# Later S5 and convolution steps, joined transposes and one shared last block in a two-layer hybrid encoder trunk

## The chip, the cores and the metric

The kernel runs on one core of one Trainium2 chip. The metric is the device time of one execution in microseconds (us), taken as the median of several runs. TensorE is called PE here, VectorE DVE, ScalarE ACT, GpSimd POOL and SyncE SP, as in the profile.

## The reference, cut to what matters

```python
for l in range(2):                                   # x: 256 tokens x 1024 channels, float32
    x = x + 0.5 * swiglu(rmsnorm(x), w_gate, w_up, w_down)      # d_ff = 2816
    h = rmsnorm(x); p = h @ w_in                     # 2048 branch columns, 4096 gate columns
    y_a = s5_mixer(u_a)        # block-diagonal complex scan, gelu, glu
    y_b = pool_mixer(u_b)      # trailing means over 2, 4, 8, 16 tokens, one 64x64 product each
    y_c = rwkv7_mixer(...)     # delta-rule state, here in chunks of 64 tokens
    y_d = b_g * conv3(c_g * z_in)
    merged = sum over g of sigmoid(gate_g) * (y_g @ w_branch[g])
    x = x + merged @ w_out
    x = x + 0.5 * swiglu(rmsnorm(x), w_gate, w_up, w_down)
return rmsnorm(x)
```

swiglu(h) is (silu(h @ w_gate) * (h @ w_up)) @ w_down.

## The kernel before

**The large products.** The 256 tokens are two token tiles t of 128. Each weight matrix comes from HBM in units of 128 x 1024 numbers (`raw`, five buffers, issued on SP). A unit is split into two float32r parts: ACT writes the rounded part `wh` (line 250), DVE the rest `wl` (line 225, called from `Unit.finish`). The activations are split in the same way into `xh` and `xl` (or `hh`, `hl` behind the feed-forward's middle, `yh`, `yl` of a branch, and `mo`). One step of the contraction over 128 rows for one token tile, called a k-step below, is three matmuls (lines 256 to 258): `wh` by `xh`, `wl` by `xh`, `wh` by `xl`, each 512 columns wide. A unit normally serves four k-steps: two k for two token tiles.

**The order.** `Flow` lays out the whole instruction order by hand when the program is built. The list of its steps holds the large products, two k-steps in each. All else hangs on generators ("threads") that wait for a place in that list: `wA(n)` runs n steps later ahead of the products, `wB(n, banks)` n steps later behind them, `wM(n, banks)` and `wT(n)` after n k-steps, at most one `M` thread for each k-step. `banks` is the number of free PSUM banks that it also asks for. Four PSUM banks of tag `pb` serve all small products, and are handed out in turn (names such as `gm`, `tmA`, `sT`, `inv`). Each engine then works through its own list strictly in that order.

**Feed-forward (`ffn`).** The columns of w_gate and w_up go in blocks of 512; since 2816 is 5 x 512 + 256, the last block of each is 256 wide, in units of four k. `act` applies silu to a gate block, `hid` multiplies it with the up block into `hd`, turns `hd` on PE with four transposes (line 268), and splits the result into `hh` and `hl`. `down` multiplies these with w_down; at its end `next_input` adds to `x`, turns each half of `x` with four transposes (line 268), and writes the scaled halves `xg`, `xh`, `xl` for the next stage. In `hid` and `next_input` the transposes of a token tile follow one step after its result, and the two token tiles end one step apart.

**Mixer (`mixer`).** `cols` multiplies the branch columns, and four threads work beside the large products: `rwkv`, `conv`, `s5`, `pool`. In `s5` the steps on PE are `sT`, `sS`, `sY` and `glu`; on DVE they are the chain `gA`, `gt`, `gB` with two scans (line 1372), then `Hs`. In `conv` the product `zc` of `cg` and `z_in` is followed by the taps `cv` (line 1497). In `rwkv` PE makes `gm` (from `W` and `BK`), turns `W` and `KB` into `tmA` and `tmB`, makes `akv`, and then climbs a ladder of four rungs that inverts a triangular matrix: `inv` from `Tm` and `Bl`, copied by ACT to `Xm`, then `inv` from `Xm` and `Rd`, which DVE adds to `Tm` and turns into `Rd` again. `Gm` is the masked `gm`, `RH` and `UV` are copies of `tmA`. The gates and the projections of the branches (`gate_steps(b)`, `branch_steps(b)`, summed in `mg`) follow in the order 3 (conv), 1 (pool), 0 (S5), 2 (RWKV).

Of the kernel before, what the change touches and what calls it, by code (L numbers as in the profile page):

```python
# [50 lines left out]
def wA(n=1):  # L51

    return ("A", n, 0)
# [7 lines left out]
def wB(n=0, banks=0):  # L61

    return ("B", n, banks)
# [7 lines left out]
def wM(n=1, banks=0):  # L71

    return ("M", n, banks)


class Flow:
# [19 lines left out]
    def spawn(self, gen):  # L96
        self.threads.append([None, gen])
        self._advance(self.threads[-1])
# [73 lines left out]
def trunk_kernel(ctx: ExitStack, tc: tile.TileContext, a, out, dbg=None):  # L172
    nc = tc.nc
    ve, sc, gp, pe = nc.vector, nc.scalar, nc.gpsimd, nc.tensor
    sp = nc.sync
# [12 lines left out]
    spawn = fl.spawn  # L188
# [15 lines left out]
    def xs(tl, t):  # L204
        return tl[:, :, t * 128:(t + 1) * 128]
# [7 lines left out]
    def free(n=1):  # L213
        fl.banks += n
        assert fl.banks <= NB
# [14 lines left out]
    class Unit:  # L230


        def __init__(self, W, k0, nk, c0, n, eng=ve):
            self.spec = (W, k0, nk, c0, n)
            self.k0, self.nk, self.eng = k0, nk, eng

        def can_load(self):
            return True
# [1 line left out]
        def load(self):  # L240
            W, k0, nk, c0, n = self.spec
            self.r = block(raw, nk, n, F32, "raw")
            sp.dma_start(out=self.r,
                         in_=W[k0 * 128:(k0 + nk) * 128, c0:c0 + n].rearrange("(k p) f -> p k f", p=128))

        def convert(self):
            W, k0, nk, c0, n = self.spec
# [12 lines left out]
    def mmu(ps, lh, ll, u, ktot):  # L260
        for k in range(u.nk):
            kk = u.k0 + k
            mm3(ps, lh(kk), ll(kk), u.h[:, k], u.l[:, k], kk == 0, kk == ktot - 1)
            fl.tick()
# [5 lines left out]
    def lxh(t):  # L270
        return lambda k: xh[:, k, t * 128:(t + 1) * 128]

    def lxl(t):
        return lambda k: xl[:, k, t * 128:(t + 1) * 128]


    rstd = {}
# [19 lines left out]
    def next_input(t, hf, p, scale, ss, gain):  # L297

        if p is not None:
            yield wA(1)
            update(t, hf, p, scale)
        yield wB(1 if p is not None else 0, 1)
        b = bank()
        transposes(b, x[t][:, hf * 512:(hf + 1) * 512], 4)
        yield wA(1)
        xg = scr.tile([128, 4, 128], F32, name="xg", tag="xg", bufs=2)
        r, n = vrow[gain[0]]
        r += gain[1] * n + 4 * hf  # L310
        tt(xg, b.rearrange("p (a q) -> p a q", q=128), vec[:, r:r + 4].unsqueeze(2).to_broadcast([128, 4, 128]))
        free()
        dh, dl = xs(xh, t)[:, 4 * hf:4 * hf + 4], xs(xl, t)[:, 4 * hf:4 * hf + 4]
        sc.activation(dh, xg, AF.Copy)  # L314
        yield wT(1)
        tt(dl, xg, dh.bitcast(F32), ALU.subtract)
        yield wA(1 if p is not None else 4)
        square_sum(t, hf, ss)
        if hf:
            rsqrt_mean(t, ss)  # L320
# [72 lines left out]
    def ffn(l, which, final=False, extra=None, first=None):  # L393
        Wg, Wu, Wd = (a[f"ffn{which}_w_{n}"][l] for n in ("gate", "up", "down"))
        st = {}
        es = ExitStack()

        def enter():
            fp = es.enter_context(tc.tile_pool(name=f"ffn{l}{which}", bufs=1))
            st["fp"] = fp  # L400
            st["hh"] = [fp.tile([128, F // 128, 128], F32R, name=f"hh{t}") for t in range(2)]
            st["hl"] = [fp.tile([128, F // 128, 128], F32R, name=f"hl{t}") for t in range(2)]
            if final:
                fin["pool"] = fp
                fin["pre"] = {}
                fin["gb"] = fp.tile([128, D], F32, name="gb")
                sp.dma_start(out=fin["gb"], in_=a["final_norm"].partition_broadcast(128))
            if first:
                first(fp)
            if extra:  # L410
                spawn(extra(fp))

        fl.step(enter, work=False)
        if first:
            for _ in range(4):
                fl.step(fl.tick)

        def act(t, pg, n, sl):
            yield wA(1)
            sg = st["fp"].tile([128, 512], F32, name="sg", tag="sg", bufs=2)  # L420
            sc.activation(sg[:, :n], pg[:, :n], AF.Silu, scale=rstd[t])  # L421
            sl[t] = sg

        def hid(t, pu, c0, n, sl):
            yield wA(1)
            sg = sl[t]
            hd = st["fp"].tile([128, 512], F32, name="hd", tag="hd", bufs=2)
            ve.scalar_tensor_tensor(out=hd[:, :n], in0=pu[:, :n], scalar=rstd[t], in1=sg[:, :n],  # L428
                                    op0=ALU.mult, op1=ALU.mult)
            k0, nk = c0 // 128, n // 128  # L430
            yield wB(1, 1)
            b = bank()
            transposes(b, hd, nk)
            yield wA(1)
            split(st["hh"][t][:, k0:k0 + nk], st["hl"][t][:, k0:k0 + nk],
                  b[:, :n].rearrange("p (a q) -> p a q", q=128))
            free()

        for c0 in range(0, F, 512):
            n = min(512, F - c0)  # L440
            P, sl = {}, {}

            def go(w, t, u, P=P, sl=sl, c0=c0, n=n):
                def f():
                    if (w, t) not in P:
                        P[w, t] = acc()
                    mmu(P[w, t][:, :n], lxh(t), lxl(t), u, 8)
                    if u.k0 + u.nk == 8:
                        spawn(act(t, P[w, t], n, sl) if w == 0 else hid(t, P[w, t], c0, n, sl))
                fl.step(f, [u])  # L450

            for w, W in enumerate((Wg, Wu)):
                nk = 1024 // n
                cuts = list(range(0, 8, nk))
                if first and c0 == w == 0:
                    cuts[1:1] = [1]
                for k0, k1 in zip(cuts, cuts[1:] + [8]):
                    u = Unit(W, k0, k1 - k0, c0, n, gp if c0 == w == 0 and k0 == 2 and not first else ve)
                    for t in range(2):
                        go(w, t, u)  # L460
        down(Wd, F // 128, lambda t: (lambda k: st["hh"][t][:, k]), lambda t: (lambda k: st["hl"][t][:, k]), 0.5,
             None if final else ("mix_norm", l) if which == 1 else ("ffn1_norm", l + 1))
        if final:
            fin["close"] = es.close
        else:
            fl.step(es.close, work=False)
# [323 lines left out]
    def mixer(l):  # L790
# [62 lines left out]
        def win(c0):  # L853
            return lambda k0: Unit(Win, k0, 2, c0, 512)

        class LowRank:

            nk = 2

            def __init__(self, k0):  # L860
                self.k0 = k0
# [460 lines left out]
        def s5():  # L1322
            yield from until("ua")
            yield wA(1)
            pu = got["ua"]
# [9 lines left out]
            U8 = et([128, G, 32], "U8")  # L1335
            sp.dma_start(out=U8, in_=ud.rearrange("g h i b -> (h i) g b"))

            yield wM(14, 1)
            sT = bank("sT").rearrange("p (u s) -> p u s", u=4)
            for u in range(4):  # L1340
                for q in range(4):
# [74 lines left out]
            pg = bank("glu").rearrange("p (j t) -> p j t", j=2)  # L1416
# [8 lines left out]
            for j in range(2):  # L1425
                ve.scalar_tensor_tensor(out=ya[:, j].rearrange("p b i -> p i b"),
                                        in0=y5[:, j].rearrange("p (i b) -> p i b", i=8), scalar=0.5,
                                        in1=in5[:, j].rearrange("p (i b) -> p i b", i=8), op0=ALU.mult, op1=ALU.mult)
# [47 lines left out]
        def conv():  # L1476
            yield from until("z_in")
            yield wA(1)
            zin = e2("zin")
            sc.activation(zin, got["z_in"], AF.Copy)  # L1480
            free()
            yield from until("bg")
            yield wA(1)
            bg = e2("bg")
            sc.activation(bg, got["bg"], AF.Copy)
            free()
            yield from until("cg")
            yield wA(1)
            zc = e2("zc")
            tt(zc, got["cg"], zin)  # L1490
            free()
            yield wA(1)
            cv = e2("cv")
            for j in range(2):
                sc.activation(cv[:, j], zc[:, j], AF.Copy, scale=col(l, "conv_w", 4 + j))
                for w in (1, 0):
                    ve.scalar_tensor_tensor(out=cv[:, j, 2 - w:], in0=zc[:, j, :S - 2 + w],  # L1497
                                            scalar=col(l, "conv_w", 2 * w + j), in1=cv[:, j, 2 - w:],
                                            op0=ALU.mult, op1=ALU.add)
                yield wA(1)  # L1500
            tt(cv, cv, bg)
            yield wA(1)
            ysplit(3, cv)
            dump("yd", cv)
# [72 lines left out]
        cols(("ua", "ub"), win(0))  # L1577
        cols(("v", "z_in"), win(1024))
        cols(("bg", "cg"), win(1536))
        gate_steps(3)  # L1580
        branch_steps(3, first=True)
        gate_steps(1)
        branch_steps(1)
        gate_steps(0)
        branch_steps(0)
        gate_steps(2, (0,))
# [103 lines left out]
```

## Time and profile before

| | us |
|---|---|
| median of three runs (1261.27 to 1264.36) | 1261.57 |
| the profiled execution, its own time | 1261.19 |
| its span, first to last instruction | 1259.3 |
| PE busy | 1238.6 (98%) |
| DVE busy | 763.9 (61%) |
| ACT busy | 618.3 (49%) |
| POOL busy | 365.6 (29%) |

The stretches of the span are, by the places of their instructions: first feed-forward to about 205 us, first mixer to about 440, second feed-forward to about 625, then the same again for the second layer. A matmul's row in the trace begins when it starts and ends when its results are written, so neighbours overlap; the cost of a matmul is read from start to start.

### The profile page before, as it was taken

The numbers are of one execution on the slowest core, as the hardware profiler recorded it, in microseconds if no ns is written. First come the engines' busy times: TensorE is split into PE (matmuls) and PEld (weight loads), VectorE is DVE, ScalarE is ACT, GpSimd is POOL, SyncE is SP. The second block draws the span as 40 slices with busy tenths as digits, with TensorE's granted clock in tenths as the row PEclk, the third lists the DMA queues.
The fourth block names the chain that finished last, engine by engine and source line by source line (L and its number), as shares of the span: only waits on it lengthen the run. The fifth ranks groups of instructions, "written<-read, shape, count | busy, mean of one in ns | idle before, by whom it ended". The sixth has DMA issues, their size and how long they took to land.

```text
span 1259.3 us, 19258 instructions
## 1 busy us (share of the span) xinstructions
PE 1238.6 (98%) x7472; PEld 1010.2 (80%) x7472; DVE 763.9 (61%) x943; ACT 618.3 (49%) x787; POOL 365.6 (29%) x504
## 2 busy tenths in 40 slices
PE   8999999998999999999999999999999999999997
PEld 6888878876778888888888888888777788888886
DVE  6955656488457665554465565464974576555543
ACT  5454445665435464453454444366554355544443
POOL 4594383154123010000069454204422221000001
PEclk9999999999999999999999999999999999999999
DMA  8676655544435566666666666556344456666661
GB/s 256 176 224 178 184 167 175 176 130 143 134 120 180 177 178 191 190 177 191 187 185 195 172 178 191 165 180 177 107 145 136 134 183 186 198 185 178 181 194 66
DMA packets 139667, 216.29 MB, mean 172 GB/s; under 512 B 30092, under 2 KB 42232, under 8 KB 139576
## 3 DMA queue, kind: packets, MB, share of 16 engines
q1 hardware_dynamic: 138296, 213.63, 57.2%
q10 hardware_dynamic: 1120, 1.40, 0.3%
q8 instruction: 58, 0.95, 0.3%
q0 software_dynamic: 160, 0.05, 0.1%
q14 instruction: 33, 0.27, 0.1%
HBM read 212.29 MB, written 1.57 MB: 170 GB/s over the span
## 4 chain that ended last, share of the span: by engine, by line
PE 93%; DVE 5%; issue 1%; ACT 1%; DMA 0%; POOLq 0%; SPq 0%; POOL 0%; DVEq 0%; ACTq 0%
PE acc L256 29%; PE acc L258 28%; PE acc L257 28%; PE pb L268 3%; DVE wl L225 1%; PE inv L1096 1%; DVE cv L1497 0%; DVE W L225 0%; PE pb L770 0%; DVE rk L1025 0%; PE wu L1201 0%; DVE Gm L225 0%; DMA vr<-in_ffn_norm_dram 0%; PE lr L945 0%; PE pb L766 0%
## 5 line engine op out<-in xcount | busy, mean ns | idle before, releaser
L225 DVE TENSOR_TENSOR wl<-raw,wh 128x1024 fp32r<-128x1024 f32 (+1 forms) x398 | 506.4, 1274 | 298.4 <-ACT wh L250 296.2
L250 ACT ACTIVATE wh<-raw 128x1024 fp32r<-128x1024 f32 (+1 forms) x393 | 414.7, 1056 | 414.0 <-PE acc L258 395.0
L256 PE MATMUL acc<-wh,xh 128*128 128x512 f32 (+1 forms) x1216 | 479.5, 394 | 0.0
L257 PE MATMUL acc<-wl,xh 128*128 128x512 f32 (+1 forms) x1216 | 462.9, 381 | 0.3 <-DVE wl L225 0.3
L258 PE MATMUL acc<-wh,xl 128*128 128x512 f32 (+1 forms) x1216 | 463.1, 381 | 0.0
L256 PEld LDWEIGHTS acc<-wh,xh 128*128 128x128 f32 x1216 | 230.1, 189 | 45.2 <-issue 4.3
L258 PEld LDWEIGHTS acc<-wh,xl 128*128 128x128 f32 x1216 | 229.8, 189 | 44.3
L257 PEld LDWEIGHTS acc<-wl,xh 128*128 128x128 f32 x1216 | 230.4, 189 | 39.4 <-DVE wl L225 0.8
L258 PE MATMUL acc<-wh,hl 128*128 128x512 f32 x352 | 138.9, 395 | 0.0
L256 PE MATMUL acc<-wh,hh 128*128 128x512 f32 x352 | 138.4, 393 | 0.0
L257 PE MATMUL acc<-wl,hh 128*128 128x512 f32 x352 | 138.0, 392 | 0.0
L225 POOL TENSOR_TENSOR wl<-raw,wh 128x1024 fp32r<-128x1024 f32 x3 | 7.2, 2388 | 253.7 <-ACT wh L250 253.7
L256 PEld LDWEIGHTS acc<-wh,hh 128*128 128x128 f32 x352 | 66.1, 188 | 15.1 <-issue 1.3
L257 PEld LDWEIGHTS acc<-wl,hh 128*128 128x128 f32 x352 | 66.2, 188 | 14.6
L258 PEld LDWEIGHTS acc<-wh,hl 128*128 128x128 f32 x352 | 66.3, 188 | 13.3
L428 DVE SCALAR_TENSOR_TENSOR hd<-acc,rs,sg 128x512 f32<-128x512 f32 (+1 forms) x48 | 33.8, 703 | 38.3 <-PE acc L258 36.4
L333 POOL TENSOR_SCALAR pre<-ss 128x1 f32<-128x1 f32 x2 | 0.4, 221 | 173.7 <-ACT junk L281 173.7
L221 ACT ACTIVATE hh<-pb 128x512 fp32r<-128x512 f32 (+1 forms) x48 | 27.0, 563 | 45.6 <-PE pb L268 45.6
L222 DVE TENSOR_TENSOR hl<-pb,hh 128x512 fp32r<-128x512 f32 (+1 forms) x48 | 31.0, 646 | 28.2 <-ACT hh L221 27.8
L421 ACT ACTIVATE sg<-acc,rs 128x512 f32<-128x512 f32 (+1 forms) x48 | 31.0, 652 | 17.8 <-PE acc L258 17.1
L225 POOL TENSOR_TENSOR mg<-mg,gate 128x512 f32<-128x512 f32 x16 | 29.6, 1863 | 30.9 <-DVE gate L225 30.9
L314 ACT ACTIVATE xh<-xg 128x512 fp32r<-128x512 f32 x24 | 15.2, 632 | 30.1 <-DVE xg L225 30.0
(349 smaller groups left out, 1154.5 us busy)
## 6 DMA issues: line engine op xcount, KB each, us to landing
raw<-in_w_in_dram SPq DMA_DIRECT2D x96, 512.0 KB
raw<-in_ffn_w_up_dram SPq DMA_DIRECT2D x88, 512.0 KB
raw<-in_ffn_w_down_dram SPq DMA_DIRECT2D x88, 512.0 KB
raw<-in_ffn_w_gate_dram SPq DMA_DIRECT2D x87, 512.0 KB
raw<-in_w_branch_dram SPq DMA_DIRECT2D x16, 512.0 KB
raw<-in_w_out_dram SPq DMA_DIRECT2D x16, 512.0 KB
x<-in_x_dram SPq DMA_DIRECT2D x2, 512.0 KB
raw<-in_rwkv_g_dram SPq DMA_DIRECT2D x8, 128.0 KB
```

Source lines behind the costliest of these rows:

```text
L221: sc.activation(dh, src, AF.Copy)
L222: eng.tensor_tensor(out=dl, in0=src, in1=dh.bitcast(F32), op=ALU.subtract)
L225: eng.tensor_tensor(out=o, in0=i0, in1=i1, op=op)
L250: sc.activation(self.h, self.r, AF.Copy)
L256: pe.matmul(ps, lhsT=lh, rhs=wh, start=first, stop=False)
L257: pe.matmul(ps, lhsT=lh, rhs=wl, start=False, stop=False)
L258: pe.matmul(ps, lhsT=ll, rhs=wh, start=False, stop=last)
L268: pe.transpose(b[:, j * 128:(j + 1) * 128], src[:, j * 128:(j + 1) * 128], ident)
L314: sc.activation(dh, xg, AF.Copy)
L421: sc.activation(sg[:, :n], pg[:, :n], AF.Silu, scale=rstd[t])
L428: ve.scalar_tensor_tensor(out=hd[:, :n], in0=pu[:, :n], scalar=rstd[t], in1=sg[:, :n], op0=ALU.mult, op1=ALU.mult)
L1096: pe.matmul(p[qs, u], lhsT=lhs[qs, u], rhs=rhs[qs, u], start=True, stop=True)
```

## The change

Four edits, all in the order or the cutting of the work:

- `hid` and `next_input` hold the transposes of the first token tile back by one step, so that those of both token tiles are asked for at the same place.
- The last 256 columns of w_gate and the last 256 of w_up are laid side by side in one unit of two k by 512 columns (two transfers for each unit), and go through one 512-wide product. `both` then runs `act` and `hid` on the two halves of its result.
- In `s5` the first PE step `sT` is asked for 38 k-steps after its place before, where it was 14; in `conv` the taps begin 14 steps after `zc` instead of 1.
- The gates and projections follow in the order 1 (pool), 3 (conv), 0, 2.

```diff
-        def __init__(self, W, k0, nk, c0, n, eng=ve):
+        def __init__(self, W, k0, nk, c0, n, eng=ve, beside=None):
...
-            sp.dma_start(out=self.r,
-                         in_=W[k0 * 128:(k0 + nk) * 128, c0:c0 + n].rearrange("(k p) f -> p k f", p=128))
+            Ws = (W,) if self.beside is None else (W, self.beside)
+            m = n // len(Ws)
+            for i, W_ in enumerate(Ws):
+                sp.dma_start(out=self.r[:, :, i * m:i * m + m],
+                             in_=W_[k0 * 128:(k0 + nk) * 128, c0:c0 + m].rearrange("(k p) f -> p k f", p=128))
...
-        yield wB(1 if p is not None else 0, 1)
+        yield wB(2 - t if p is not None else 0, 1)
         b = bank()
         transposes(b, x[t][:, hf * 512:(hf + 1) * 512], 4)
...
-            yield wB(1, 1)
+            yield wB(2 - t, 1)
             b = bank()
             transposes(b, hd, nk)
...
+        def both(t, p, c0, sl):
+            yield from act(t, p, sl, 256)
+            yield from hid(t, p[:, 256:], c0, 256, sl)
...
-                    mmu(P[w, t][:, :n], lxh(t), lxl(t), u, 8)
+                    mmu(P[w, t], lxh(t), lxl(t), u, 8)
                     if u.k0 + u.nk == 8:
-                        spawn(act(t, P[w, t], n, sl) if w == 0 else hid(t, P[w, t], c0, n, sl))
+                        spawn(both(t, P[w, t], c0, sl) if n < 512 else
+                              act(t, P[w, t], sl) if w == 0 else hid(t, P[w, t], c0, n, sl))
...
-            for w, W in enumerate((Wg, Wu)):
-                nk = 1024 // n
-                cuts = list(range(0, 8, nk))
+            for w, W in enumerate((Wg, Wu) if n == 512 else (Wg,)):
+                cuts = list(range(0, 8, 2))
...
-            yield wM(14, 1)
+            yield wM(38, 1)
             sT = bank("sT").rearrange("p (u s) -> p u s", u=4)
...
             tt(zc, got["cg"], zin)
             free()
-            yield wA(1)
+            yield wA(14)
             cv = e2("cv")
...
+        gate_steps(1)
+        branch_steps(1, first=True)
         gate_steps(3)
-        branch_steps(3, first=True)
-        gate_steps(1)
-        branch_steps(1)
+        branch_steps(3)
         gate_steps(0)
         branch_steps(0)
```

The first place is DVE in each mixer, between the last `BK` and the second pair of `Gm`. Before:

```order
L225 TENSOR_TENSOR BK<-kp,L_2543 128x4x128
L225 TENSOR_TENSOR gA<-sS,TC 128x512
L225 TENSOR_TENSOR gt<-sS,TS 128x512
L225 TENSOR_TENSOR gB<-sX,TC 128x512
L225 TENSOR_TENSOR gB<-gB,gt 128x512
L222 TENSOR_TENSOR yl_2674<-yb,yh_2673 128x512
L225 TENSOR_TENSOR wl<-raw,wh 128x1024
L225 TENSOR_TENSOR gt<-sX,TS 128x512
L225 TENSOR_TENSOR gA<-gA,gt 128x512
L1372 SCALAR_TENSOR_TENSOR gB<-R_615,gB 128x512
L225 TENSOR_TENSOR wl<-raw,wh 128x1024
L225 TENSOR_TENSOR zc<-cg,zin 128x512
```

The seven S5 entries between `BK` and `zc` have left this place. The same place of DVE in the changed kernel, as far as the copies of `tmA`:

```order
L225 TENSOR_TENSOR BK<-kp,L_2497 128x4x128
L222 TENSOR_TENSOR yl_2594<-yb,yh_2593 128x512
L225 TENSOR_TENSOR wl<-raw,wh 128x1024 x2
L225 TENSOR_TENSOR zc<-cg,zin 128x512
L225 TENSOR_TENSOR Gm_2658<-gm,cst 128x512
L225 TENSOR_TENSOR Gm_2664<-gm,cst 128x512
L225 TENSOR_TENSOR wl<-raw,wh 128x1024
L225 TENSOR_TENSOR Gm_2698<-gm,cst 128x512
L225 TENSOR_TENSOR Gm_2704<-gm,cst 128x512
L225 TENSOR_TENSOR wl<-raw,wh 128x1024 x2
L1130 COPY RH<-tmA 64x4x64
```

`zc` now stands right behind `yl` and two `wl`, and no `cv` stands among the `Gm`.

The second place is DVE in the ladder of each mixer, from the first turn of `Rd` into `Tm` (or, after the change, the second entry behind it) to the first sum into `Tm`. Before:

```order
L1131 STREAM_TRANSPOSE Tm<-Rd 128x256
L1409 TENSOR_SCALAR in_2981<-in_2981 128x512
L225 TENSOR_TENSOR in_2981<-in_2981,y_2967 128x512
L225 TENSOR_TENSOR mg_3016<-acc,gate 128x512
L225 TENSOR_TENSOR wl<-raw,wh 128x1024
L225 TENSOR_TENSOR mg_3046<-acc,gate 128x512
L1414 SCALAR_TENSOR_TENSOR y_2967<-in_2981,y_2967 128x512
L225 TENSOR_TENSOR mg_3079<-acc,gate 128x512
L225 TENSOR_TENSOR wl<-raw,wh 128x1024
L225 TENSOR_TENSOR mg_3108<-acc,gate 128x512
L225 TENSOR_TENSOR Tm<-inv,Tm 128x256
```

The three entries of the end of S5 (`in`, `in`, `y`) have left, and others have come in. After:

```order
L225 TENSOR_TENSOR wl<-raw,wh 128x1024
L1505 SCALAR_TENSOR_TENSOR cv<-zc,vec,cv 128x255
L1505 SCALAR_TENSOR_TENSOR cv<-zc,vec,cv 128x254
L225 TENSOR_TENSOR mg_2945<-acc,gate 128x512
L1505 SCALAR_TENSOR_TENSOR cv<-zc,vec,cv 128x255
L1505 SCALAR_TENSOR_TENSOR cv<-zc,vec,cv 128x254
L225 TENSOR_TENSOR Hs<-gA,gB 128x16x31
L225 TENSOR_TENSOR mg_2981<-acc,gate 128x512
L225 TENSOR_TENSOR wl<-raw,wh 128x1024
L225 TENSOR_TENSOR cv<-cv,bg 128x512
L225 TENSOR_TENSOR mg_3011<-acc,gate 128x512
L225 TENSOR_TENSOR Tm<-inv,Tm 128x256
```

The five entries of `cv` and the `Hs` now stand ahead of the sum into `Tm`, and so does, further up between the last `RH` and the first `Tm`, the whole S5 chain that was taken from the first place.

## Rows read from the trace of the kernel before

**Rows 1.** The page's group of ACT's `wh`; then PE's waits over the span.

```profile
L250 ACT ACTIVATE wh<-raw 128x1024 fp32r<-128x1024 f32 (+1 forms) x393 | 414.7, 1056 | 414.0 <-PE acc L258 395.0
...
PE gm L1065 <- DVE zc L225: 3.6, 2, 1.8
PE tmB L1118 <- ACT UV L1125: 2.7, 2, 1.4
```

**Rows 2.** Timeline of PE, first mixer: start us, us, engine, line, operation.

```profile
278.95 1.16 PE L1065 MATMUL gm<-W,BK 64*128 64x128 f32 x16
...
282.99 0.48 PE L1065 MATMUL gm<-W,BK 64*128 64x128 f32 x2
...
286.75 0.79 PE L256 MATMUL acc<-wh,xh 128*128 128x512 f32 x1
...
289.42 0.40 PE L256 MATMUL acc<-wh,xh 128*128 128x512 f32 x1
...
292.19 0.27 PE L1117 MATMUL tmA<-cst,W 128*128 128x128 f32 x1
```

**Rows 3.** Busy by stretch: PE, PEld, DVE, ACT, POOL, granted clock, DMA share, GB/s.

```profile
285.93:289.34 3.41, 3.41 (x14) 2.70 (x11) 3.38 (x5) 3.23 (x4) 2.89 (x3) 0.50 0.40 142
```

**Rows 4.** Timeline of DVE in the same stretch.

```profile
274.98 1.21 DVE L225 TENSOR_TENSOR wl<-raw,wh 128x1024 fp32r<-128x1024 f32 x1
...
276.72 0.68 DVE L225 TENSOR_TENSOR gA<-sS,TC 128x512 f32<-128x512 f32 x1
...
284.56 0.69 DVE L225 TENSOR_TENSOR zc<-cg,zin 128x512 f32<-128x512 f32 x1
285.15 1.22 DVE L1372 TENSOR_TENSOR_SCAN gA<-R,gA 128x512 f32<-128x512 f32 x1
```

**Rows 5.** Timeline of PE: two S5 steps that move, and a later product.

```profile
264.20 1.08 PE L1343 MATMUL sT<-LS,U 128*32 128x128 f32 x32
...
268.32 0.66 PE L1352 MATMUL sS<-cst,sN 128*128 128x128 f32 x4
...
277.73 0.39 PE L257 MATMUL acc<-wl,xh 128*128 128x512 f32 x1
```

**Rows 6.** Timelines of POOL and of DVE while POOL multiplies `gB`, and after it.

```profile
287.69 1.47 POOL L225 TENSOR_TENSOR gB<-gB,TS 128x512 f32<-128x512 f32 x1
...
287.46 1.97 DVE L1497 SCALAR_TENSOR_TENSOR cv<-zc,vec,cv 128x255 f32<-128x255 f32 x2
...
290.54 0.99 DVE L1497 SCALAR_TENSOR_TENSOR cv<-zc,vec,cv 128x255 f32<-128x255 f32 x2
```

**Rows 7.** The chain that ended last, in the ladder: start us, us, what.

```profile
299.63 0.23 PE acc L256
...
300.33 1.01 PE sY L1388 x32
...
316.90 1.73 PE glu L1419 x8
...
320.01 0.38 PE inv L1096 x32
```

**Rows 8.** Timeline of PE, last block: first and last of 22 narrow matmuls.

```profile
131.16 0.28 PE L258 MATMUL acc<-wh,xl 128*128 128x256 f32 x1
...
133.68 0.28 PE L258 MATMUL acc<-wh,xl 128*128 128x256 f32 x1
```

**Rows 9.** Timeline of PE around four transposes alone, and around eight in a row.

```profile
80.29 0.39 PE L258 MATMUL acc<-wh,xl 128*128 128x512 f32 x1
...
81.65 0.40 PE L258 MATMUL acc<-wh,xl 128*128 128x512 f32 x1
...
83.48 0.40 PE L258 MATMUL acc<-wh,xl 128*128 128x512 f32 x1
...
657.75 0.40 PE L258 MATMUL acc<-wh,xl 128*128 128x512 f32 x1
...
660.01 0.39 PE L258 MATMUL acc<-wh,xl 128*128 128x512 f32 x1
```

More of the change, by code (lines that the diff above doesn't have):

```diff
@@ L230, in trunk_kernel @@
     class Unit:
-        def __init__(self, W, k0, nk, c0, n, eng=ve):
+        def __init__(self, W, k0, nk, c0, n, eng=ve, beside=None):
             self.spec = (W, k0, nk, c0, n)
-            self.k0, self.nk, self.eng = k0, nk, eng
+            self.k0, self.nk, self.eng, self.beside = k0, nk, eng, beside
         def can_load(self):
@@ L416, in ffn, with act @@
                 fl.step(fl.tick)
-        def act(t, pg, n, sl):
+        def act(t, pg, sl, n=512):
             yield wA(1)
@@ L427, in hid @@
             hd = st["fp"].tile([128, 512], F32, name="hd", tag="hd", bufs=2)
-            ve.scalar_tensor_tensor(out=hd[:, :n], in0=pu[:, :n], scalar=rstd[t], in1=sg[:, :n],
+            ve.scalar_tensor_tensor(out=hd[:, :n], in0=pu, scalar=rstd[t], in1=sg[:, :n],
                                     op0=ALU.mult, op1=ALU.mult)
             k0, nk = c0 // 128, n // 128
-            yield wB(1, 1)
+            yield wB(2 - t, 1)
             b = bank()
@@ L457, in ffn @@
                 for k0, k1 in zip(cuts, cuts[1:] + [8]):
-                    u = Unit(W, k0, k1 - k0, c0, n, gp if c0 == w == 0 and k0 == 2 and not first else ve)
+                    u = Unit(W, k0, k1 - k0, c0, 512, gp if c0 == w == 0 and k0 == 2 and not first else ve,
+                             None if n == 512 else Wu)
                     for t in range(2):
```

## The prediction

> **What bounds the kernel now.** I read the page first, then PE's waits, then the timelines of the place where PE waits. TensorE is busy through almost the whole span, and the chain that ended last runs along it, so a change counts only where it takes work or waiting off PE. Weights are not late: nearly all idle time of ACT before it splits a block was ended by a product that freed a buffer, not by a transfer [rows 1]. Inside the span, PE has two waits worth naming, each once in each mixer: `gm` for `zc` (1.8 us) and `tmB` for `UV` (1.35 us each, 2.7 in all) [rows 1].
>
> The first costs more than its length. Between the starts of the two `gm` groups lie four k-steps and a group, 282.99 - 278.95 = 4.04 us; from the second to `tmA` lie six k-steps and a group, which at 0.2267 us for a matmul (below) should be 4.04 + 1.36 = 5.40 us, and took 292.19 - 282.99 = 9.20 us [rows 2]. So 3.80 us were lost: 1.8 us of wait and 2.0 us behind it, where the granted clock was 0.50, that is 1.2 GHz instead of 2.4, for 3.41 us [rows 3]. Six matmuls in it took 289.42 - 286.75 = 2.67 us instead of 1.36, a loss of 1.31 us [rows 2]. Before the clock fell, PE had stood idle for 1.8 us. With the 1.35 us of `tmB`, a mixer loses 5.15 us.
>
> `zc` was late because DVE works through its list without a pause: from 276.72 to 284.56 it did seven pieces of S5, one `yl` and two `wl` before `zc` [rows 4]. A 128x512 product costs 285.15 - 284.56 = 0.59 us, a `wl` about 1.14 us (1.21 in the row, less the overlap with the next) [rows 4], so `yl` and two `wl` are 2.87 us and the S5 pieces 7.84 - 2.87 = 4.97 us.
>
> **The shared last block.** Each of the four feed-forwards has 2 matrices x 2 token tiles x 8 k x 3 = 96 matmuls of 256 columns; they become 48 of 512. Twenty-one starts of the narrow kind take 133.68 - 131.16 = 2.52 us, 0.1200 us each [rows 8]; six of the wide kind take 81.65 - 80.29 = 1.36 us, 0.2267 us each [rows 9]. A pair saves 0.0133 us, and 192 pairs 2.56 us, all on PE. The cost by the rows cannot be below nothing, since the columns are the same. SP issues eight transfers of half the size per feed-forward instead of four; they hide behind blocks loaded ahead, as the ends of ACT's idle time show [rows 1]. Silu and `hid` now follow each other, one step more before a PSUM accumulator is free; its next user comes four k-steps (2.7 us) after the `hid` may start, against one half-width ACT pass and one half-width DVE product, an estimated 0.4 us each, so I cost it at nothing; without that cover it is about 1 us per feed-forward.
>
> The Trainium skill puts this gain lower (TensorE: Matmul & The Clock Gate, Back-to-back issue gap): at full clock an isolated matmul costs its columns plus about 2.5 ns. By that, 192 matmuls fewer would save 0.48 us. Here the rows show 0.0133 us a pair, about five times as much, and they decide.
>
> **The joined transposes.** Four transposes alone add 83.48 - 81.65 - 1.36 = 0.47 us to six matmuls; the one place where eight stand in a row adds 660.01 - 657.75 - 1.36 = 0.90 us [rows 9]. Joining two groups saves 0.04 us. There are 20 pairs for `hd` and 10 for `x`, and four pairs of half length, which I count as half: 1.3 us. The ends are nothing and 1.7 us. For `x`, the first token tile's halves become ready 1.36 us later and are wanted four k-steps (2.7 us) after the joined eight, while DVE has two 0.59 us products before the first `xl` and ACT one pass beside them; I cost this at nothing, with about 1 us to spare.
>
> **The moved S5 and convolution, first place.** The S5 pieces leave DVE ahead of `zc`, so `zc` ends at about 276.7 + 2.9 + 0.6 = 280.2. `sT` and `sS` leave PE before `gm`, so PE arrives 1.08 + 0.66 = 1.7 us sooner [rows 5], at about 281.3 for the second `gm`: the wait of 1.8 us goes, and with it the half clock. `RH` and `UV` no longer queue behind `cv`, so the `tmB` wait goes too; if not, 1.35 us a mixer come back. But a new wait is next: the product at 277.73 uses the `wl` that ended at 274.98 + 1.21 = 276.19 [rows 4, 5], a margin of 1.54 us, and PE comes 1.7 us or a little more sooner (the rows' widths leave out the gap around a group). DVE's list up to there has not changed, so PE waits 0.2 to 0.6 us; I take 0.4.
>
> Behind `sT` in the list of DVE nothing else waits that PE needs before the ladder. The pool branch, now first, has its `yl` done before `zc`, some 20 k-steps ahead of its use; the convolution's result is done by the third rung and that of S5 soon after the fourth, each more than 25 k-steps ahead.
>
> **The moved steps, second place: the ladder.** The chain and the taps now stand on DVE between `RH` and the first sum into `Tm`, and PE's second rung needs that sum. PE takes, from the end of `tmB`, 320.01 - 299.63 = 20.38 us to that rung, less `sY` (1.01) and `glu` (1.73), which leave this stretch: 17.6 us [rows 7]. DVE starts with `RH` at the same moment. Its list: S5 pieces 4.97 us, the second scan 1.14 (like a `wl`), four `wl` 4.56, four `mg` and the product of `cv` with `bg` 2.95, `Hs` 0.6, two pairs of `cv` 1.8 [rows 4, 6], four half-width entries (`RH` twice, `Tm` twice) at an estimated 0.4 each, 1.6: together 17.6 us. So the cover is just used up before anything disturbs it.
>
> It is disturbed. While POOL multiplied `gB` (1.47 us), a pair of `cv` on DVE took 1.97 us against 0.99 alone [rows 6]. In the new order the same two POOL products start when the second scan ends, and meet a `wl` and the first `cv`; then POOL's next product (`Bl`, half as wide) meets the second `cv`. A bound from below is nothing, from above two whole products, 2.9 us. The nearest row says 1 us for one product; with two and a half I take 2.0 us. PE thus waits about 2.0 us at the second rung in each mixer. That is more than the 1.8 us after which the clock fell, so I expect half clock behind it. Its price lies between nothing and 2.0 us; I take the 1.31 us of the six matmuls [rows 2], since small products fill the rest here.
>
> **How the numbers follow.** Per mixer 5.15 us leave, and 0.4 + 2.0 + 1.31 = 3.7 us come: 1.45 us gained, 2.9 for both. With 2.56 and 1.3 the sum is 6.8 us. The profiled execution took 1261.19 us, 0.38 below the median of the runs; off the median this gives **1254.8 us**. Chance 0.38.
>
> The rivals:
>
> - *The wait without half clock.* Against it stands the fall after 1.8 us; for it, that none followed the 1.35 us of `tmB`. 2 x 1.31 us less: 1252.2 us, chance 0.25.
> - *The ladder's cover holds*, because POOL and DVE do not meet as I think. Only 0.4 us a mixer remain: 2.56 + 1.3 + 2 x 4.75 = 13.4 us off, 1248.2 us, chance 0.20. The equal 17.6 us on both sides speak for it, the `cv` pair against.
> - *Narrow matmuls cost only their columns and a small constant.* The shared block gives 0.5 instead of 2.56 us: 1256.9 us, chance 0.02, as the rows contradict it; this is what the skill's figure above would mean here.
> - *The wait only changes its place.* At the upper ends, 0.5 + 2.9 + 2.0 = 5.4 us a mixer against 5.15, the two mixers give back 0.5 us and 3.4 remain: 1258.2 us, chance 0.11. This is the case in which the move does not do what it is for.
> - *Slower: the rungs fall behind one after another.* The other three rungs hold the rest of S5 and its `wl`. If DVE's list between two sums were longer than PE's rung (about 8 us without `glu`), each would repeat the wait and the half clock: 6 x 3.3 = 20 us, 1274.7 us. It decides from 8 us on; I count some 3 to 5 us there. Chance 0.04.
>
> The range is 1248.0 to 1257.8 us: it takes in the first four cases and leaves out 0.15. A difference of 0.3% (3.8 us) is about what a measurement of this kernel can tell from no change; below 1257.8 us lie the first four cases. Faster 0.85, within 0.3% 0.11, slower 0.04.
>
> **What would show it.** In the changed profile: no wait of `gm` for `zc` or of `tmB` for `UV`; a wait of `inv` for `Tm` near 2 us in each mixer with a stretch at 0.50 clock behind it; a wait below 1 us for a `wl` just before the first `gm`; rows of 128x256 gone, and eight transposes at 0.90 us. Wrong would be a wait of PE at the turn of a stage for `xl` (the joined `x`), for a transfer in the last block, or a rung other than the second that waits.

## The result, and the profile after

The changed kernel takes **1254.12 us** in the median of 4 runs (1253.45 to 1254.76), against 1261.82 us for the kernel before, measured beside it: a ratio of 0.9938, with a 95% interval of 0.9925 to 0.9951. The prediction was 1254.8 us (1248.0 to 1257.8). The profiled execution took 1254.47 us, its span 1252.7 us (before 1261.19 and 1259.3).

PE still fills the span, with 192 matmuls fewer and 4.9 us less busy. The page's busy time by engine:

```profile
PE 1233.7 (98%) x7280; PEld 999.8 (80%) x7280; DVE 763.5 (61%) x943; ACT 617.8 (49%) x787; POOL 368.9 (29%) x504
```

PE's waits (tile and releaser: us in total, times, longest us) answer to the two waits of [rows 1]:

```profile
PE inv L1104 <- DVE Tm L225: 3.5, 2, 1.8
PE acc L260 <- DVE wl L225: 1.1, 3, 0.4
...
PE inv L1104 <- DVE Tm L1139: 0.5, 2, 0.2
```

`gm` for `zc` and `tmB` for `UV` are gone. In their place stand, in each mixer, 1.76 us before the second rung, 0.41 us for a `wl` and 0.24 us before the first rung.

The timeline of PE in the first mixer answers to [rows 2] and [rows 7] (start us, us, engine, line, operation, in brackets the idle time before and its releaser). The ends of PE's rows are modelled by the profile, so only their starts are compared:

```profile
276.36 0.83 PE L1073 MATMUL gm<-W,BK 64*128 64x128 f32 x10
...
280.44 0.38 PE L1073 MATMUL gm<-W,BK 64*128 64x128 f32 x2
...
286.99 0.27 PE L1125 MATMUL tmA<-cst,W 128*128 128x128 f32 x1
...
309.43 0.40 PE L261 MATMUL acc<-wh,xl 128*128 128x512 f32 x1
311.58 0.45 PE L1104 MATMUL inv<-Tm,Bl 32*32 32x32 f32 x32 [1.76 <-DVE Tm L225]
...
313.88 0.80 PE L259 MATMUL acc<-wh,xh 128*128 128x512 f32 x1
314.47 0.63 PE L260 MATMUL acc<-wl,xh 128*128 128x512 f32 x1
...
316.29 0.43 PE L1396 MATMUL sY<-LK,U 128*32 128x128 f32 x8
```

From the second `gm` to `tmA` it is now 6.55 us (before 9.20), though `sT` (about 1.2 us with its gap) has come into this stretch. Behind the wait, matmuls start 0.43 to 0.59 us apart in place of 0.2267. That is half clock, as the granted clock of two stretches shows (the third number from the end of a row, behind the busy times of the five engines):

```profile
308.86:312.27 3.41, 1.65 (x38) 1.11 (x37) 3.38 (x6) 1.58 (x2) 0.00 (x0) 1.00 0.32 79
312.27:315.69 3.42, 3.42 (x39) 2.34 (x38) 2.49 (x3) 0.38 (x1) 1.14 (x1) 0.50 0.47 138
```

DVE's timeline shows why the sum into `Tm` is late:

```profile
292.04 0.42 DVE L1130 COPY RH<-tmA 64x256 f32<-64x256 f32 x1 [0.17 <-PE tmA L1125]
...
302.23 1.61 DVE L225 TENSOR_TENSOR wl<-raw,wh 128x1024 fp32r<-128x1024 f32 x1
303.77 2.31 DVE L1505 SCALAR_TENSOR_TENSOR cv<-zc,vec,cv 128x255 f32<-128x255 f32 x2
...
306.60 0.99 DVE L1505 SCALAR_TENSOR_TENSOR cv<-zc,vec,cv 128x255 f32<-128x255 f32 x2
...
311.02 0.41 DVE L225 TENSOR_TENSOR Tm<-inv,Tm 128x256 f32<-128x256 f32 x1
```

POOL's timeline shows what DVE met there:

```profile
301.47 1.29 POOL L225 TENSOR_TENSOR gA<-gA,TC 128x512 f32<-128x512 f32 x1 [11.38 <-DVE gA L1380]
302.71 2.30 POOL L225 TENSOR_TENSOR gB<-gB,TS 128x512 f32<-128x512 f32 x1
```

From `RH` to the sum DVE has no pause and needs 311.02 - 292.04 = 18.98 us. Beside POOL's products the `wl` took 1.61 us, others 1.22, and the first `cv` pair 2.31 us, the second 0.99.

Eight transposes now stand in a row (this answers to [rows 9]): 60.91 - 59.11 less four matmuls of 0.2267 leaves 0.89 us.

```profile
59.11 0.39 PE L261 MATMUL acc<-wh,xl 128*128 128x512 f32 x1
59.34 1.03 PE L271 MATMUL pb<-cst,hd 128*128 128x128 f32 x8
...
60.91 0.40 PE L259 MATMUL acc<-wh,xh 128*128 128x512 f32 x1
```

**Where the time went, by stage.** The table cuts each profiled span at starts in PE's timeline: the first `acc`, the `zA` of each mixer, the `oT` near the end of each mixer, the end. F1 is the first feed-forward, F2 the two between the mixers, F3 the last one with the tail. Each row is one execution, the profiled one.

| kernel | to the first `acc` | F1 | mixer 1 | F2 | mixer 2 | F3 |
|---|---|---|---|---|---|---|
| before | 8.92 | 210.67 | 166.77 | 453.27 | 166.81 | 252.86 |
| shared block alone | 9.20 | 209.56 | 166.75 | 452.26 | 168.21 | 252.39 |
| joined transposes alone | 9.54 | 210.54 | 166.77 | 452.87 | 168.15 | 252.60 |
| moves alone | 9.66 | 210.08 | 163.84 | 453.30 | 165.26 | 252.88 |
| **changed** | 8.77 | 209.56 | 165.31 | 451.67 | 165.30 | 252.06 |
| taps later | 9.46 | 210.28 | 161.96 | 451.66 | 162.01 | 251.84 |
| no POOL products | 9.83 | 209.66 | 162.47 | 451.64 | 162.50 | 251.91 |
| S5 alone | 9.89 | 209.33 | 162.41 | 451.67 | 162.42 | 252.04 |
| taps alone | 9.27 | 209.98 | 165.19 | 451.64 | 165.21 | 251.83 |
| product later | 9.09 | 210.09 | 163.26 | 451.68 | 163.34 | 251.99 |
| small waits | 9.50 | 209.09 | 161.62 | 451.66 | 161.60 | 251.63 |

The last seven share the code of all feed-forwards. There F2 repeats within 0.04 us, F3 within 0.43, but the start and F1 vary by 1.1 and 1.2 us, with the first loads. So single mixers and F2 are the places to read a tenth of a us; F3 and the medians are not. Changed against before: F2 1.60, mixers 1.46 and 1.51, F3 0.80, start and F1 1.26 us: 6.63 us of span.

### The profile page after: what moved, and what is told of

It reads as the page before. It is cut to its first block, busy times and chain, and to the rows that moved or that the text cites. A ratio compares the mean times of both kernels' runs of the same rounds, so it can differ in the third digit from the quotient of the medians.

```text
span 1252.7 us, 18891 instructions
## 1 busy us (share of the span) xinstructions
PE 1233.7 (98%) x7280; PEld 999.8 (80%) x7280; DVE 763.5 (61%) x943; ACT 617.8 (49%) x787; POOL 368.9 (29%) x504
## 4 chain that ended last, share of the span: by engine, by line
PE 93%; DVE 5%; issue 1%; ACT 0%; DMA 0%; POOLq 0%; SPq 0%; POOL 0%; DVEq 0%; ACTq 0%
PE acc L259 29%; PE acc L260 28%; PE acc L261 28%; PE pb L271 3%; DVE wl L225 1%; PE inv L1104 1%; DVE cv L1505 0%; DVE mg L225 0%; PE pb L778 0%; DVE rk L1033 0%; PE gm L1073 0%; PE sY L1396 0%; PE wu L1209 0%; DMA vr<-in_ffn_norm_dram 0%; PE lr L953 0%
## 5 line engine op out<-in xcount | busy, mean ns | idle before, releaser
L259 PE MATMUL acc<-wh,xh 128*128 128x512 f32 x1152 | 465.1, 404 | 0.0
L260 PE MATMUL acc<-wl,xh 128*128 128x512 f32 x1152 | 450.8, 391 | 1.1 <-DVE wl L225 1.1
L261 PE MATMUL acc<-wh,xl 128*128 128x512 f32 x1152 | 451.0, 392 | 0.0
L259 PEld LDWEIGHTS acc<-wh,xh 128*128 128x128 f32 x1152 | 217.1, 188 | 48.4 <-issue 4.5
L261 PEld LDWEIGHTS acc<-wh,xl 128*128 128x128 f32 x1152 | 217.0, 188 | 46.5
L260 PEld LDWEIGHTS acc<-wl,xh 128*128 128x128 f32 x1152 | 217.4, 189 | 43.6 <-DVE wl L225 2.5
L221 ACT ACTIVATE hh<-pb 128x512 fp32r<-128x512 f32 (+1 forms) x48 | 24.4, 561 | 42.2 <-PE pb L271 42.2
L1525 ACT ACTIVATE gate<-acc,rs 128x512 f32<-128x512 f32 x32 | 22.0, 688 | 15.9 <-PE acc L261 15.6
```

Of the source, the lines that this page charges most:

```text
L221: sc.activation(dh, src, AF.Copy)
L259: pe.matmul(ps, lhsT=lh, rhs=wh, start=first, stop=False)
L260: pe.matmul(ps, lhsT=lh, rhs=wl, start=False, stop=False)
L261: pe.matmul(ps, lhsT=ll, rhs=wh, start=False, stop=last)
L1525: sc.activation(g_, P[t], AF.Sigmoid, scale=rstd[t])
```

## The experiments

Each ratio is to the kernel before, run beside the group: 1261.52 us beside the first four kernels, 1263.38 beside the next four, 1262.88 beside the last. Kernels of different groups are best compared by stage.

**The shared block alone** (the kernel before with the parts of `Unit`, `act`, `hid` and the loop over `c0`):

```diff
+        def both(t, p, c0, sl):
...
+            for w, W in enumerate((Wg, Wu) if n == 512 else (Wg,)):
```

> The kernel before with the shared last block alone. Theory (a matmul pays a constant of 0.0133 us beside its columns): 192 x 0.0133 = 2.6 us off, near 1259.2 us; matmuls of 128x256 gone, 192 fewer on PE, the waits of gm for zc (1.8 us) and of tmB for UV (1.35 us) as before. Rival 1 (the constant is some 2.5 ns): 0.5 us off, near 1261.3 us. Rival 2 (the accumulator of the last block comes free too late, or its transfers): a new wait of PE behind the block, no gain or a loss of up to 1 us per feed-forward.

Measured: 1259.87 us beside 1261.52 us before (ratio 0.9980, 0.9971 to 0.9990). F2 fell by 1.01 us for two feed-forwards and F3 by 0.47: 0.5 us each. No wait came behind the block. The block itself shows the gain, in the second feed-forward from its first matmul to the first of w_down (before, first two lines; this kernel, last two).

```profile
557.88 0.28 PE L256 MATMUL acc<-wh,xh 128*128 128x256 f32 x1
...
570.26 0.39 PE L256 MATMUL acc<-wh,hh 128*128 128x512 f32 x1
```

```profile
557.03 0.39 PE L259 MATMUL acc<-wh,xh 128*128 128x512 f32 x1
...
568.87 0.39 PE L259 MATMUL acc<-wh,hh 128*128 128x512 f32 x1
```

It took 12.38 us and takes 11.83, in the fourth feed-forward too. In the first and the third, where twelve small matmuls of the mixer stand in the block (`vb` and `BB`), it took 13.57 and takes 13.07 and 13.08. That is 2.1 us in all. So the shared block gains, but less than 0.64 us each. One cause is in these rows: four transposes among narrow matmuls (before, first three lines) and among wide ones (this kernel, last three).

```profile
128.50 0.28 PE L258 MATMUL acc<-wh,xl 128*128 128x256 f32 x1
128.62 0.60 PE L268 MATMUL pb<-cst,hd 128*128 128x128 f32 x4
...
129.65 0.28 PE L258 MATMUL acc<-wh,xl 128*128 128x256 f32 x1
```

```profile
127.97 0.40 PE L261 MATMUL acc<-wh,xl 128*128 128x512 f32 x1
128.20 0.60 PE L271 MATMUL pb<-cst,hd 128*128 128x128 f32 x4
...
129.79 0.39 PE L261 MATMUL acc<-wh,xl 128*128 128x512 f32 x1
```

Less six matmuls, the first is 1.15 - 0.72 = 0.43 us, the second 1.82 - 1.36 = 0.46. Two such groups lie in each last block, so widening it costs 0.06 us back, 0.24 in all. The twelve small matmuls likewise cost 1.19 us among narrow ones and 1.24 among wide ones, 0.1 in all. Of 2.56 that leaves 2.2; the last 0.1 us is not explained. By the Trainium skill's 2.5 ns for an isolated matmul at full clock (TensorE: Matmul & The Clock Gate, Back-to-back issue gap) the gain would be an estimated 0.5 us in all; 2.1 us for 192 pairs, 11 ns each, do not agree with it.

The second mixer got 1.40 us longer, though nothing was edited there. Its two waits in PE's timeline:

```profile
903.48 1.16 PE L1073 MATMUL gm<-W,BK 64*128 64x128 f32 x14 [1.83 <-DVE zc L225]
...
916.88 0.48 PE L1126 MATMUL tmB<-cst,KB 128*128 128x128 f32 x1 [2.78 <-ACT UV L1133]
```

The granted clock behind the first and behind the second:

```profile
904.53:907.94 3.41, 3.41 (x16) 2.81 (x16) 3.37 (x6) 2.81 (x3) 3.27 (x4) 1.00 0.35 133
...
916.70:920.11 3.41, 3.23 (x18) 2.47 (x22) 2.12 (x3) 1.59 (x4) 2.88 (x4) 0.51 0.52 155
```

Here no half clock followed the 1.83 us of `gm`. PE then came sooner to `tmB` and waited 2.78 us for the same `UV`, in place of 1.36; half clock followed that wait. From the second `gm` to `tmA` it took 7.62 us here and 9.20 in the first mixer, where the half clock came, so there it cost 1.58 us. So in the kernel before, the half clock behind `gm` was hidden by the wait of `tmB`, and only their sum counted.

**The joined transposes alone** (`wB(2 - t, 1)` at both places):

```diff
-            yield wB(1, 1)
+            yield wB(2 - t, 1)
```

> The kernel before with the joined transposes alone. Theory: 0.04 us for each of 30 pairs and four half pairs, 1.3 us off, near 1260.5 us, eight transposes at 0.90 us in place of twice 0.47 us. Rival 1: the later halves of the joined x cost as much as the joining gives, no change (1261.8 us). Rival 2: PE waits for xl at the turn of a stage, up to 1 us at each of ten places: slower, up to 1270 us.

Measured: 1260.95 us (ratio 0.9994, 0.9985 to 1.0003). The median can't tell this from nothing, because the second mixer again got longer by 1.34 us, with a wait of 2.77 us of `tmB`. F2 can: it fell by 0.40 us, 0.2 us a feed-forward, 0.8 in all (F3 fell by 0.26, less than it varies by itself). On top of the shared block (changed against shared alone) F2 falls by 0.59, 1.2 in all. No wait for `xl` appeared.

**The moves alone** (the branches in the order of the change too):

```diff
-            yield wM(14, 1)
+            yield wM(38, 1)
...
-            yield wA(1)
+            yield wA(14)
```

> The kernel before with the moves in the mixer alone (S5 at 38 in place of 14 steps, the taps at 14 in place of 1, the pool branch first). Theory: what the changed kernel gained beyond 2.6 + 1.3 us comes from here: 3 to 4 us off, 1258 to 1259 us, with a wait of inv for Tm of about 1.8 us in each mixer and half clock behind it. Rival 1: the moves give only 1 to 2 us (1260 to 1261), the other parts more than was reckoned. Rival 2: the wait before the second rung needs the other parts too (joined transposes make PE arrive sooner): then no wait here and 8 us or more off (1253 us or less).

Measured: 1256.80 us (ratio 0.9959, 0.9946 to 0.9971), 4.7 us off, more than the 3 to 4 expected. Both mixers waited 1.8 us for `Tm`, as in the changed kernel, but in the profiled execution half clock followed only in the second. PE's wait in the first mixer:

```profile
312.99 0.45 PE L1096 MATMUL inv<-Tm,Bl 32*32 32x32 f32 x32 [1.78 <-DVE Tm L225]
```

The granted clock behind it, and behind the wait of the second mixer:

```profile
312.40:315.80 3.40, 2.81 (x72) 2.17 (x73) 3.37 (x6) 1.57 (x3) 0.65 (x1) 1.00 0.52 158
...
930.80:934.30 3.50, 3.50 (x40) 2.39 (x39) 2.47 (x3) 0.38 (x1) 1.18 (x1) 0.51 0.44 131
```

That prices the half clock by itself: 165.31 - 163.84 = 1.47 us (changed against this, mixer 1), and 165.26 - 163.84 = 1.42 us within this kernel.

**The taps later:**

```diff
-            yield wA(14)
+            yield wA(20)
```

> The changed kernel with the taps of the convolution at 20 in place of 14, which puts them and the product with bg (3.9 us of DVE) behind the second rung's sum into Tm. Theory (the second rung waits because DVE's list is longer than PE's way there, and the clock falls behind the wait): both waits of 1.76 us go, and the half clock with them, another 1 to 1.3 us each: 5.5 to 6.1 us below the changed kernel, 1248 to 1248.6 us. Rival 1 (the clock's price is small): 3.5 us, 1250.6 us. Rival 2 (the wait only changes its place, to the third rung or to the branch that reads the convolution): within 1 us of the changed kernel, 1253 to 1255 us, with a new wait of 1.5 us or more in the profile.

Measured: 1248.78 us (ratio to before 0.9893, 0.9879 to 0.9906). The rung no longer waits, no stretch between the start and the tail has half clock, and each mixer is 3.3 us shorter (165.31 to 161.96): 1.76 of wait and 1.59 left, where the half clock was priced at 1.42 to 1.47. PE's waits that remain in the mixers:

```profile
PE acc L260 <- DVE wl L225: 0.8, 2, 0.4
PE inv L1104 <- DVE Tm L1139: 0.5, 2, 0.2
```

The second rung in PE's timeline, with no wait beside it:

```profile
311.12 0.45 PE L1104 MATMUL inv<-Tm,Bl 32*32 32x32 f32 x32
```

**Without POOL's two products:**

```diff
-            tt(gA, gA, TC, eng=gp)
-            tt(gB, gB, TS, eng=gp)
```

> The changed kernel without the two products gA by TC and gB by TS that POOL forms behind the scans (3.6 us of POOL); that part of S5 is left out. Theory (POOL's products slow DVE's list: wl 1.61 in place of 1.22, the cv pair 2.31 in place of 0.99, 1.7 us together, which is the wait): the wait of 1.76 us at the second rung shrinks to 0.1 to 0.6 us and no half clock follows, 1254.1 - 2 x (1.2 to 1.7 + 1.45) = 1248 to 1249 us. Rival (DVE's list is by itself longer than PE's way to the rung, POOL has no part): the wait stays above 1.4 us, 1253 to 1254 us.

Measured: 1249.72 us (ratio 0.9891, 0.9878 to 0.9905). That is 0.7 us above the forecast; but the mixers fell from 165.31 to 162.47 us, 2.84, as 1.34 of wait and 1.47 of clock would have it. The wait at the rung shrank from 1.76 to 0.4 us, and the clock stayed full. The wait:

```profile
PE inv L1104 <- DVE Tm L225: 0.8, 2, 0.4
```

DVE's timeline, with the lines that answer to those of the changed kernel:

```profile
293.17 0.42 DVE L1130 COPY RH<-tmA 64x256 f32<-64x256 f32 x1 [0.17 <-PE tmA L1125]
...
303.36 1.21 DVE L225 TENSOR_TENSOR wl<-raw,wh 128x1024 fp32r<-128x1024 f32 x1
304.49 1.38 DVE L1503 SCALAR_TENSOR_TENSOR cv<-zc,vec,cv 128x255 f32<-128x255 f32 x2
...
310.81 0.42 DVE L225 TENSOR_TENSOR Tm<-inv,Tm 128x256 f32<-128x256 f32 x1
```

310.81 - 293.17 = 17.64 us, against 18.98 with the products: 1.34 us, all of it in the `wl` (0.40) and the first `cv` pair (0.93). The pair is still 0.39 us over the other, beside POOL's `Bl`. To the end of the sum the list is 18.05 us, while PE was ready for the rung 17.8 us after `RH` began, in the changed kernel (311.58 - 1.76 - 292.04 = 17.78) as here. So even without POOL the list is a little too long, which is the 0.4 us that remain. The Trainium skill (SBUF — State Buffer, Who interferes with whom) says that DVE and GpSimd share a port pair which one instruction holds to its end; that DVE is longer just beside POOL's products, by up to 1.3 us, agrees with it.

**S5 moved alone** (with the order of the branches):

```diff
-            yield wA(14)
+            yield wA(1)
```

> The changed kernel with the taps back at 1, so that S5 alone is moved. Theory: no wait of gm for zc, since it was the S5 pieces that stood ahead of zc; no wait at the second rung, since the cv pieces (3.9 us) are off that list; tmB waits for UV again because cv is back between the Gm and RH, 0 to 1.35 us a mixer: 1248.8 to 1251.5 us. Rival 1 (S5 alone overfills the ladder): a wait of 1 us or more at the second rung, 1252 to 1254 us. Rival 2 (the scans, not cv, made UV late): no wait of tmB, 1248.8 us or less.

Measured: 1249.63 us (ratio 0.9894, 0.9881 to 0.9908). No wait at the second rung, as the theory has it, but none of `tmB` either (Rival 2): with S5 gone, `cv` between the `Gm` and `RH` does not make `UV` late. The first rung waits longer instead.

```profile
PE inv L1104 <- DVE Tm L1139: 1.4, 2, 0.7
```

**The taps moved alone** (with the order of the branches):

```diff
-            yield wM(38, 1)
+            yield wM(14, 1)
```

> The changed kernel with S5 back at 14, so that the taps and the order of the branches alone are moved. Theory: the wait of gm for zc (1.8 us) and the half clock behind it stay, the wait of tmB goes, the wl before the first gm and the second rung do not wait: 2 x (1.85 + 1.45 - 0.65) = 5.3 us above the kernel without a wait at the rung (1248.8), 1254 us. Rival (the branch order frees zc too, since the pool's yl and the products stand elsewhere): no wait of gm, 1249 us. Rival 2 (the taps make the second rung wait also without S5): both waits, 1258 us or more.

Measured: 1254.12 us (ratio 0.9929, 0.9916 to 0.9941). The wait of `gm` and the half clock behind it stay, and `tmB` does not wait. PE's wait, then the granted clock of the stretch behind it in the first mixer:

```profile
PE gm L1073 <- DVE zc L225: 3.7, 2, 1.8
```

```profile
285.26:288.67 3.41, 3.41 (x19) 2.80 (x16) 3.41 (x5) 0.00 (x0) 2.55 (x2) 0.50 0.45 159
```

So S5's move frees `zc`, and the taps' does not; `UV` is in time with either; and the wait at the rung needs both. The new order of the branches stands in both kernels, and no run has it by itself. DVE's list speaks for the moves: ACT's `UV` waits for DVE's `RH`, and from `zc` to the first `RH` DVE took 12.31 us before, 10.13 with S5 alone, where a scan and `Hs` are gone and no `cv` meets POOL, and 8.59 with the taps alone, where `cv` is gone.

**Only the product of `cv` with `bg` later:**

```diff
+            yield wA(6)
             tt(cv, cv, bg)
```

> The changed kernel with only the product of cv with bg (0.6 us of DVE) put behind the second rung's sum. Theory (the wait follows the list's length, and a wait of some 1.2 us is followed by no fall of the clock, as none followed 1.35 us before the change): the wait falls from 1.76 to about 1.16 us, no half clock, 1254.1 - 2 x (0.6 + 1.45) = 1250.0 us. Rival 1 (half clock follows the shorter wait too): 1252.9 us. Rival 2 (the wait does not follow the list): 1254 us.

Measured: 1250.86 us (ratio 0.9903, 0.9888 to 0.9919). 0.6 us taken from DVE's list took 0.6 us from the wait (1.76 to 1.16), and the clock stayed at 1.00 behind it. The rung in PE's timeline, then the stretch behind it:

```profile
311.84 0.45 PE L1104 MATMUL inv<-Tm,Bl 32*32 32x32 f32 x32 [1.16 <-DVE Tm L225]
```

```profile
312.20:315.60 3.40, 3.40 (x73) 2.38 (x65) 2.22 (x2) 0.38 (x1) 1.16 (x1) 1.00 0.70 236
```

The mixer fell from 165.31 to 163.26 us: 2.05, of which 0.6 is wait and 1.45 clock.

**A better version, the small waits:**

```diff
-            yield wM(38, 1)
+            yield wM(14, 1)
             sT = bank("sT")
...
-            yield wM(4, 1)
+            yield wM(32, 1)
             sS = bank("sS")
...
-            yield wA(14)
+            yield wA(20)
```

> The kernel with the taps at 20 and, beside it, S5 cut in two: its first product (sT) back at 14, ahead of the first gm, the transposes sS and all behind them where DVE reaches them after the first Tm (32 steps on). Theory (the waits of 0.41 us for wl and of 0.24 us for the first Tm in each mixer come from PE's arriving early, and sT, 1.24 us on PE, put ahead of them costs the same work elsewhere): both waits go, no new one comes, 2 x 0.65 = 1.3 us below 1248.8, near 1247.5 us. Rival 1 (the ladder, now 1.2 us shorter on PE, waits at the second rung again): a wait of 0.3 us or more there, 1248 to 1250 us; with half clock 1251 us or more. Rival 2 (zc is late again because of sT's return): a wait of gm, 1250 us or more.

Measured: **1246.76 us** (1246.45 to 1248.05; ratio to before 0.9874, 0.9858 to 0.9891), the fastest here. But the mixers explain only 0.34 and 0.41 us of it against the taps later; the rest is F3 (0.21) and above all F1 (1.19), which vary by themselves. The `wl` no longer waits, and 0.5 us a mixer stand again at the rungs, a part of Rival 1:

```profile
PE inv L1104 <- DVE Tm L1139: 0.6, 2, 0.3
PE inv L1104 <- POOL Bl L225: 0.4, 2, 0.2
```

## Why the prediction was right

The time came out 0.7 us from the forecast. That it came so near is in part luck: the mixers, the shared block and the joined transposes give 6.2 us by the table below, 6.8 were forecast, and the two medians differ by 7.7, with a start and an F1 that vary by over a us each. The terms, read by stage, hold as follows:

| term | predicted, us | measured, us | from |
|---|---|---|---|
| shared last block | 2.56 | 2.1 | length of the block, shared block alone |
| joined transposes | 1.3 | 0.8 to 1.2 | F2, joined alone, and on top of the shared block |
| one mixer, gain | 1.45 | 1.46 and 1.51 | stages, changed against before |
| leaves a mixer | 5.15 | 5.3 | the gain and the new terms, added up |
| new: `wl` before the first `gm` | 0.4 | 0.41 | waits |
| new: second rung | 2.0 | 1.76 | waits |
| new: half clock behind it | 1.31 | 1.42 to 1.47 | changed against moves alone |
| new, not named: first rung | 0 | 0.24 | waits |

- *Shared block.* Mis-sized by 0.5 us. The step that failed took 0.0133 us from plain runs of matmuls and left out that transposes and small matmuls among narrow ones are cheaper (0.43 against 0.46 us for four transposes). The last 0.1 us stays open.
- *Joined transposes.* Eight in a row cost 0.89 us, as read from [rows 9], yet the stages give 0.2 to 0.3 us a feed-forward and not 0.33. The direction holds, the size was at the upper end. No cover failed in the changed kernel: no wait for `xl` and none in the last block. (With the taps alone, PE waited once for `x`, 0.58 us at the end of F1.)
- *First place.* `zc` came early, and `tmB` did not wait, as forecast. But the reason given for `tmB`, that `RH` and `UV` no longer queue behind `cv`, was half of it: with S5 moved and `cv` in its old place `UV` is in time too. And of the 2.0 us counted behind `gm`, 1.58 were half clock, and they were no loss of their own: the shared block alone showed them hidden by `tmB`'s wait. The sum of 5.15 us stood because it was read between two starts, and not added up from causes.
- *The ladder.* This is the step that carried the forecast, and the runs show it: DVE's list without POOL's products took 18.05 us, the sum counted in as the working did (17.64 to the start of the sum), where the working had 17.6; PE's way took 17.8, the working had 17.6; and the products put 1.34 us on the list, the working 2.0. So the wait came out at 1.76 and not at 1.3, because the two sides were not quite equal: 0.4 us remain without the products. The 2.0 us of the forecast are near it because a list too short and a meeting too dear offset each other. One of the prediction's own signs of being wrong did come: the first rung waits too, 0.24 us, since the S5 chain stands ahead of the first `Tm` as well, and the working reckoned only up to the second.
- *The half clock* was taken at 1.31 us in both mixers. The size is near (1.42 to 1.47), but that it follows each time is not so: it did not in the first mixer of the moves alone. It is the rival "the wait without half clock", true now and then. The changed kernel's own runs fit that: two with a mean granted clock of 0.995 took 1254.47 and 1254.76 us, two with 0.997 took 1253.45 and 1253.77.
- The cover of the ladder did not hold, and the later rungs did not fall behind one after another, so the rivals at 1248.2 and 1274.7 us fell; the upper ends at which the wait only changes its place (1258.2 us) were not reached in any term. A time near 1248.2 us is to be had by another place of the taps (1248.78 us), and with S5 moved and the taps left where they were the kernel takes 1249.63 us: within the change, the move of the taps lost 4.5 us by the medians, and 2.9 us a mixer, 5.8 in all, by the stages.

## What to carry to other kernels

When an engine's list is moved past a wait, add up the list between the new wait's two ends, and the way of the engine that waits for it: here they were 19.4 (18.98 to the start of the sum) and 17.8 us, and six tenths of a us on that list decided about two. A wait of TensorE with half clock behind it cost nearly twice its length here (1.76 and 1.47 us), so shortening it by 0.6 us already gave 2.05 of the 3.35 us a mixer that removing it gave. Read small gains from a stage's own length, since the median mixes them with a start that varies by a us.

## What was not expected of the hardware

- The fall of the clock behind a wait of TensorE is not certain. Of twelve waits of 1.75 to 1.84 us in the profiled executions of six kernels (before, shared alone, joined alone, moves alone, changed, taps alone), nine were followed by a stretch of 3.41 us at 0.50 and three were not; both of 2.77 and 2.78 us were, and none of six of 1.15 to 1.4 us was. What decides among the twelve stays open.
- The same stretch at half clock can cost 1.4 us or nothing: nothing where a later wait of the same engine for another engine takes it up, as in the kernel before.
- POOL pays for the meeting too, and by whole entries. `gB` took 2.28 to 2.30 us in the seven kernels where a `wl` ran on DVE when it began, and 1.47 to 1.49 in the three where the end of a `cv` did ([rows 6] is one); each time it ended 1.14 to 1.17 us behind that entry. `mg`, which reads the PSUM accumulator `acc`, was not longer beside `gB` than elsewhere (0.68 us; POOL, then DVE, with the taps later):

```profile
304.08 2.30 POOL L225 TENSOR_TENSOR gB<-gB,TS 128x512 f32<-128x512 f32 x1
```

```profile
305.13 0.68 DVE L225 TENSOR_TENSOR mg<-acc,gate 128x512 f32<-128x512 f32 x1
```
